# The first modulation's columns in four column groups of the array, as plain 32-bit products

## The chip, the cores and the metric

The kernel runs on one core of a Trainium2 chip. The metric is the device time of one execution in microseconds (us). The core has five engines that run beside each other and meet at semaphores: TensorE (PE in the profile, with PEld for its weight loads), VectorE (DVE), ScalarE (ACT), GpSimd (POOL) and SyncE (SP), which here issues most DMAs.

## The reference, cut to what matters

One layer of a hybrid attention and retention network over 1024 latent and 256 context tokens of width 1024. It begins with a modulation: a vector for each of the two kinds of token goes through SiLU and a 1024 x 6144 matrix, and its first two sixths shift and scale the normalised tokens, from which everything else is computed.

```python
c_silu = jax.nn.silu(c)[:, None, :]
cctx_silu = jax.nn.silu(c_ctx)[None, :]
sh1, sc1, g1, sh2, sc2, g2 = jnp.split(c_silu @ w_ada[l] + b_ada[l], 6, axis=-1)
csh1, csc1, ... = jnp.split(cctx_silu @ w_ada[l] + b_ada[l], 6, axis=-1)
hx = _modulate(_rmsnorm(x, norm1_g[l]), sh1, sc1)      # h * (1 + scale) + shift
hc = _modulate(_rmsnorm(ctx, norm1_g[l]), csh1, csc1)
(xq, xk, xv, ...) = jnp.split(hx @ w_in[l], IN_OFFSETS, axis=-1)
```

All data are 32-bit floats.

## The kernel before

Large products are made from two parts: a number is split into a high part in the format `float32r`, and the low rest, and three such products are summed (`mm3`, `chain`). A product of plain `float32` operands needs no split; the kernel uses it for small things.

The stage that matters is the start, up to about 80 us of the span. Its instructions stand in an order written out by hand (`tc.manual_schedule`), one call after the other, and each engine takes its own instructions in that order. There:

- `load_x`, `square_x`, `rstd_x`, `scale_x` bring a block of 128 tokens (ten of them) and normalise it: DMA by SP, squares on ACT, the root on POOL, the scaling on DVE. `transp` turns its 128 x 128 blocks on PE into PSUM tiles `tp`, `c0` and `c1`; `evac_t` copies some of them out.
- The two conditioning vectors stand as columns, `ccol`: 128 partitions x 8 blocks x 2 vectors. `silu_cc` puts them through SiLU on ACT.
- The modulation's columns (shift and scale) come in four groups `g`, each for two of the eight 128-wide blocks of the width. A group's weights come in four loads `load_ag(g, q)` of 512 KB. The 1024 columns of such a load hold two blocks `k` of the summed dimension, 512 result columns for each.
- `ag_mm(g, q)` multiplies: the vectors are the stationary operand, the weights stream. For groups 0 and 1 (`g < NEX`) these are plain products of two columns by 512, for groups 2 and 3 the weights are split by `ag_hi` (ACT) and `ag_lo` (DVE) into tiles `agh` and `agl`, the vectors by `split_cc` into four columns `ccr`, and two `float32r` products are made for each block.
- `ag_ev` copies the sums from PSUM (`arow`), `ag_tr` turns them into columns (a transpose for groups 0 and 1; for 2 and 3 a product with `sel`, which adds the high and low rows), and `ag_fin` adds the bias and multiplies by the gain, on DVE, into `acol`.
- With a block's shift and scale, `mod_h` (ACT), `mod_v` and `mod_l` (DVE) make the modulated block's high and low parts, and `first_mm(half, kb)` multiplies them on PE by the first weights, whose parts `split_hi` and `split_lo` make.

The last two steps need every earlier one: `first_mm(0, 0)` waits for group 0 of the modulation and for the split weights, and after it PE goes through the sixteen `first_mm` in order, with transposes, `ag_mm` and `ag_tr` between them. SP's DMAs go through eight semaphores in turn, so a load is issued when the one eight places ahead has landed, and the tile that it fills is free.

Of the kernel before, what the change touches and what calls it, by code (L numbers as in the profile page):

```python
# [8 lines left out]
F32 = mybir.dt.float32  # L9
F32R = mybir.dt.float32r  # L10
AF = mybir.ActivationFunctionType
ALU = mybir.AluOpType
# [4 lines left out]
P = 128  # L17
D = 1024
KB = D // P
# [21 lines left out]
def tile_hybrid_layer(ctx, tc: tile.TileContext, io, dbg=None):  # L41
    nc = tc.nc
    vec, act, pool, pe, sync = nc.vector, nc.scalar, nc.gpsimd, nc.tensor, nc.sync

    def sb(name, side, bufs=1):
        return tc.alloc_tile_pool(name=name, bufs=bufs, side=side, reuse_waits="tile")
# [31 lines left out]
    ident = cpool.tile([P, P], F32, name="ident")  # L78
# [72 lines left out]
    s0 = sb("start", "right")  # L151
# [12 lines left out]
    def square_x(tb):  # L164
        act.activation(s_tile("v", 1), xs[tb], AF.Square, accum_out=ssq[:, tb : tb + 1])
# [6 lines left out]
    def scale_x(tb):  # L172
        vec.tensor_scalar(xs[tb], xs[tb], rstd[:, tb : tb + 1], None, ALU.mult)
# [13 lines left out]
    def p_tile(tag):  # L187
        return p0.tile([P, 512], F32, tag=tag, bufs=2 if tag == "tp" else 3, name=tag)
# [14 lines left out]
    copy = {"act": act.copy, "vec": vec.tensor_copy}  # L203
    moved = set()

    def evac_t(grid, half, kb, eng):
        moved.add((grid, half, kb))
        x = xT[grid, kb, half]
        copy[eng](x, tps[grid, half, kb][:, : x.shape[-1]])
# [8 lines left out]
    def mod_h(grid, half, kb):  # L218
        h = hxp(0, kb, half * 512, 512) if grid else hcp(0, kb, 0, C)
        a, sh = (cx if grid else ca)[kb]  # L220
        act.activation(h, turned(grid, half, kb), AF.Identity, bias=sh, scale=a)

    def mod_v(grid, half, kb, v=None):
        modv[grid, half, kb] = s_tile("vh", 3, 512) if v is None else v
        vec.tensor_scalar(modv[grid, half, kb], turned(grid, half, kb), *(cx if grid else ca)[kb], ALU.mult, ALU.add)

    def mod_l(grid, half, kb):
        lo = low(grid, half, kb, F32R)
        h = hxp(0, kb, half * 512, 512) if grid else hcp(0, kb, 0, C)
        vec.tensor_tensor(lo, modv[grid, half, kb], h.bitcast(F32), ALU.subtract)  # L230
        (hx if grid else hc)[1][kb, half] = lo

    ccol = s0.tile([P, KB, 2], F32, name="ccol")
    cs2 = csp.tile([P, D], F32, name="cs")

    def load_cc():
        sync.dma_start(ccol, io["ccol"])

    def silu_cc():
        act.activation(ccol, ccol, AF.Silu)

    def load_bc():
        sync.dma_start(cs2, io["cvec"][0:1].to_broadcast([P, D]))
# [1 line left out]
    def silu_bc():  # L247
        act.activation(cs2, cs2, AF.Silu)

    ag, agh, agl, arow, arow_s, acolT = {}, {}, {}, {}, {}, {}
    ccr = s0.tile([P, KB, 4], F32R, name="ccr")
    sel = s0.tile([4, 2], F32, name="sel")
    NEX = 2

    def load_ag(g, q):
        ag[g, q] = s_tile("x", 14)
        sync.dma_start(ag[g, q], io["w_ada1g"][g, q])

    def ag_hi(g, q):
        agh[g, q] = s0.tile([P, D], F32R, tag="ahl", bufs=6, name="agh")
        act.copy(agh[g, q], ag[g, q])

    def ag_lo(g, q):
        agl[g, q] = s0.tile([P, D], F32R, tag="ahl", bufs=6, name="agl")
        vec.tensor_tensor(agl[g, q], ag[g, q], agh[g, q].bitcast(F32), ALU.subtract)

    def split_cc():
        act.copy(ccr[:, :, 0:2], ccol)  # L270
        vec.tensor_tensor(ccr[:, :, 2:4], ccol, ccr[:, :, 0:2].bitcast(F32), ALU.subtract)
        vec.tensor_tensor(sel, ident[:4, 0:2], ident[:4, 2:4], ALU.add)

    def ag_mm(g, q):
        if q == 0:
            arow[g] = p_tile("tp")
        for e in range(2):
            k, es = 2 * q + e, slice(e * 512, e * 512 + 512)
            if g < NEX:
                pe.matmul(arow[g][:2], ccol[:, k], ag[g, q][:, es], start=k == 0, stop=k == KB - 1)  # L280
            else:
                pe.matmul(arow[g][:4], ccr[:, k], agh[g, q][:, es], start=k == 0, stop=False)
                pe.matmul(arow[g][:4], ccr[:, k], agl[g, q][:, es], start=False, stop=k == KB - 1)

    def ag_ev(g, eng):
        n = 2 if g < NEX else 4
        arow_s[g] = s0.tile([4, 512], F32, tag="arow", bufs=1, name="arow")[:n]
        copy[eng](arow_s[g], arow[g][:n])

    def ag_tr(g):  # L290
        acolT[g] = p_tile("tp")
        for n in range(4):
            o, a = acolT[g][:, 2 * n : 2 * n + 2], arow_s[g][:, n * P : n * P + P]
            if g < NEX:
                pe.transpose(o, a, ident[:2, :2])
            else:
                pe.matmul(o, a, sel, start=True, stop=True)

    def ag_fin(g):
        kbs = slice(2 * g, 2 * g + 2)  # L300
        t = acol[:, :, kbs].rearrange("p s k i -> p i k s")
        bb = cst["b"][:, 0:16].rearrange("p (i k) -> p i k", i=2)
        vec.tensor_tensor(t, acolT[g][:, 0:8].rearrange("p (i k s) -> p i k s", i=2, k=2), bb[:, :, kbs].unsqueeze(3).to_broadcast([P, 2, 2, 2]), ALU.add)
# [20 lines left out]
    def split_lo(half, t):  # L324
        vec.tensor_tensor(first[t][half][:, 1], fraw[half, t], first[t][half][:, 0].bitcast(F32), ALU.subtract)
# [296 lines left out]
    def next_load(i):  # L622
        nraw[i] = rawload(io["w_qkv"][1, 0, i])
# [26 lines left out]
    with tc.manual_schedule():  # L650
        load_ag(0, 0)
        load_cc()
        load_x(0)
        load_x(1)
        silu_cc()
        split_cc()
# [177 lines left out]
        ag_hi(2, 2)  # L834
        ag_lo(2, 2)
        load_ag(3, 2)
        load_ag(3, 3)
        load_bc()
        load_ex()
        next_load(0)  # L840
        ag_hi(2, 3)
        ag_lo(2, 3)
        ag_mm(2, 0)
        ag_mm(2, 1)
        first_mm(1, 2)
# [3 lines left out]
        transp(7, (5,), ("tp",))  # L849
        ag_mm(2, 2)  # L850
        ag_mm(2, 3)
        ag_hi(3, 0)
        ag_lo(3, 0)
        silu_bc()
        evac_t(True, 1, 5, "act")
        ag_hi(3, 1)
        split_lo(1, 1)
        scale_x(9)
        scale_x(8)
        ag_lo(3, 1)  # L860
        ag_ev(2, "act")
        split_hi(1, 0)
        split_lo(1, 0)
        ag_hi(3, 2)
        first_mm(1, 3)
        ag_tr(2)
        ag_fin(2)
        ag_mm(3, 0)
        ag_mm(3, 1)
# [3 lines left out]
        mod_h(True, 1, 4)  # L873
        mod_v(True, 1, 4)
        mod_l(True, 1, 4)
        ag_lo(3, 2)
        ag_hi(3, 3)
        ag_lo(3, 3)
        first_mm(0, 4)
        transp(8, (2,), ("tp",))  # L880
        transp(9, (2,), ("tp",))
# [615 lines left out]
    for db in range(KB):  # L1497
# [4 lines left out]
        for half in range(2):  # L1502
# [21 lines left out]
    arow = ap_.tile([32, P], F32, name="arow")  # L1524
# [100 lines left out]
    for kb in range(KB):  # L1625
        t = wop.tile([P, 2, 512], F32R, tag="wo", bufs=KB, name="wo")
# [11 lines left out]
    for kb in (6, 7, 0, 1, 2, 3, 4, 5):  # L1638
        t = (wop if kb >= 6 else op).tile([P, 2, 512], F32R, tag="wx", bufs=2, name="wx") if kb >= 4 else None
# [475 lines left out]
```

## Time and profile before

| | us |
|---|---|
| median of three runs | 1742.88 |
| lowest and highest | 1742.45, 1744.89 |
| the profiled execution | 1742.64 |
| its span, first to last instruction | 1740.9 |
| PE, DVE, ACT, POOL busy in the span | 1721.2, 1225.3, 846.9, 537.9 |

The span leaves out 1.74 us of the execution's own time. PE is called busy in 99% of the span, but its matmuls are pipelined and the ends of them are modelled: a row of 0.39 us may be followed by the next after 0.23. How long a stream of matmuls takes is therefore read from the starts of its rows, and not from the durations. A plain 32-bit matmul of the program appears as two rows, each with a weight load of its own. In a row of the timeline the first number is the start from the span's begin, the second the duration (of a merged group, from its first start to its last end), and the bracket holds the idle time of the engine before it and what ended it.

### The profile page before, as it was taken

How to read it: one execution, taken by the hardware profiler on the slowest of the kernel's cores; microseconds unless marked ns; L12 is line 12 of the kernel's file. 1: busy time of each engine (PE TensorE's matmuls, PEld its weight loads, DVE VectorE, ACT ScalarE, POOL GpSimd, SP SyncE). 2: the span in 40 equal slices, each digit the busy share in tenths (PEclk: the TensorE clock that was granted, in tenths of full speed). 3: DMA queues.
4: the chain of work that ended last, by engine and by line, in shares of the span. 5: the costliest groups of instructions: out<-in, count | busy, mean ns of one | idle time of the engine just before them, and what ended most of it. 6: DMA issues, size and time to landing. Idle time of an engine off the chain costs nothing.

```text
span 1740.9 us, 25068 instructions
## 1 busy us (share of the span) xinstructions
PE 1721.2 (99%) x8405; PEld 1426.1 (82%) x8405; DVE 1225.3 (70%) x2460; ACT 846.9 (49%) x1803; POOL 537.9 (31%) x703
## 2 busy tenths in 40 slices
PE   8999999999999999999999999999999999999998
PEld 4788888888888887888888888888888888888886
DVE  4877887765776666765555557876888898856756
ACT  5756666563443434443444323544444444545444
POOL 1100001002343344512222211012566666421444
PEclk9999999999999999999999999999999999999999
DMA  8254445542231223578876566768666676898744
GB/s 341 84 162 146 125 144 173 157 125 49 79 89 51 80 43 94 167 260 276 267 226 233 196 196 193 256 215 224 176 197 169 187 209 167 254 318 289 242 152 178
DMA packets 141361, 313.02 MB, mean 180 GB/s; under 512 B 19024, under 2 KB 31472, under 8 KB 135024
## 3 DMA queue, kind: packets, MB, share of 16 engines
q1 hardware_dynamic: 116896, 230.40, 38.4%
q0 software_dynamic: 12032, 70.27, 18.0%
q10 hardware_dynamic: 12304, 10.75, 1.8%
q8 instruction: 66, 1.08, 0.2%
q14 instruction: 63, 0.52, 0.1%
HBM read 250.78 MB, written 121.91 MB: 214 GB/s over the span
## 4 chain that ended last, share of the span: by engine, by line
PE 81%; DMA 5%; issue 5%; DVE 4%; POOL 3%; ACT 2%; SPq 0%; POOLq 0%; ACTq 0%; DVEq 0%
PE u L1377 29%; PE mm L126 4%; PE mm L124 4%; PE mm L125 4%; PE mm L115 3%; PE mm L113 3%; PE mm L114 3%; PE y L1377 2%; PE R L514 2%; PE om L125 2%; PE om L124 2%; PE om L126 2%; PE pr L114 2%; PE pr L113 2%; PE pr L115 2%
## 5 line engine op out<-in xcount | busy, mean ns | idle before, releaser
L1377 PE MATMUL u<-T,wc 128*128 128x512 f32 x960 | 225.0, 390 | 0.3 <-ACT pu L1411 0.2
L1377 PEld LDWEIGHTS u<-T,wc 128*128 128x128 f32 x960 | 179.5, 188 | 39.7 <-ACT pu L1411 2.5
L1377 PE MATMUL y<-wc,ahl 128*128 128x512 f32 x924 | 210.1, 389 | 0.4 <-DVE wc L90 0.4
L1377 PEld LDWEIGHTS y<-wc,ahl 128*128 128x128 f32 x924 | 173.3, 188 | 36.8 <-DVE wc L90 0.8
L90 DVE TENSOR_TENSOR wc<-ur,wc 128x512 fp32r<-128x512 f32 x161 | 118.2, 737 | 62.9 <-ACT wc L89 61.0
L89 ACT CAST wc<-ur 128x512 fp32r<-128x512 f32 x161 | 99.7, 621 | 119.2 <-PE u L1377 69.3
L114 PE MATMUL mm<-low,wc 128*128 128x512 f32 (+1 forms) x312 | 119.1, 382 | 0.0
L1377 PE MATMUL u<-h2a,wc 128*128 128x512 f32 x480 | 112.4, 389 | 0.0
L113 PE MATMUL mm<-hx,wc 128*128 128x512 f32 x264 | 107.3, 406 | 0.2 <-ACT wc L627 0.2
L115 PE MATMUL mm<-hx,wc 128*128 128x512 f32 x264 | 105.7, 401 | 0.0
L1377 PEld LDWEIGHTS u<-h2a,wc 128*128 128x128 f32 x480 | 90.0, 188 | 19.2 <-DVE pu L1420 0.4
L1377 PE MATMUL u<-hxT,wc 128*128 128x512 f32 x384 | 89.6, 389 | 0.0
L585 POOL COPY pad<-pu 128x1 f32<-128x1 f32 x54 | 35.8, 662 | 166.6 <-DVE pu L1414 123.1
L585 POOL COPY pad<-st 128x1 f32<-128x1 f32 x32 | 5.9, 185 | 258.5 <-DVE st L488 258.5
L1377 PEld LDWEIGHTS u<-hxT,wc 128*128 128x128 f32 x384 | 72.1, 188 | 14.9
L89 ACT CAST wc<-raw 128x512 fp32r<-128x512 f32 x86 | 53.1, 621 | 40.1 <-PE pr L115 9.7
L90 DVE TENSOR_TENSOR wc<-raw,wc 128x512 fp32r<-128x512 f32 x86 | 60.5, 708 | 12.1 <-ACT wc L89 8.6
L126 PE MATMUL mm<-wc,low 128*128 128x512 f32 (+1 forms) x180 | 68.8, 382 | 0.0
L89 ACT CAST wc<-s 128x512 fp32r<-128x512 f32 x56 | 34.8, 622 | 68.6 <-PE u L1377 66.4
L114 PEld LDWEIGHTS mm<-low,wc 128*128 128x128 f32 x312 | 58.9, 189 | 7.1
L89 ACT CAST wc<-wr 128x512 fp32r<-128x512 f32 x56 | 34.7, 622 | 56.3 <-PE u L1377 47.2
L1377 PE MATMUL u<-hx,wc 128*128 128x512 f32 x192 | 61.9, 390 | 0.0
(412 smaller groups left out, 4752.8 us busy)
## 6 DMA issues: line engine op xcount, KB each, us to landing
d_a<-at SPq DMA_DIRECT2D x77, 256.0 KB, 6.3
ur<-d_a SPq DMA_DIRECT2D x77, 256.0 KB, 5.3
ur<-in_w_up SPq DMA_DIRECT2D x74, 256.0 KB, 5.8
d_w<-in_w_down POOLq DMA_DIRECT2D x66, 256.0 KB, 7.2
aw<-in_w_ada SPq DMA_DIRECT2D x32, 512.0 KB, 3.9
d_a<-d_a POOLq DMA_DIRECT2D x44, 256.0 KB, 7.3
ur<-d_w SPq DMA_DIRECT2D x44, 256.0 KB, 3.8
d_s<-in_w_up POOLq DMA_DIRECT2D x36, 256.0 KB, 6.0
```

Of the source, the lines that this page charges most:

```text
L89: act.copy(hi, src)
L90: (lo_eng or vec).tensor_tensor(lo, src, hi.bitcast(F32), ALU.subtract)
L113: pe.matmul(out, wh, xh, start=k == 0, stop=False)
L114: pe.matmul(out, wh, xl, start=False, stop=False)
L115: pe.matmul(out, wl, xh, start=False, stop=k == n - 1)
L124: pe.matmul(out, ah, bh, start=first, stop=False)
L125: pe.matmul(out, ah, bl, start=False, stop=False)
L126: pe.matmul(out, al, bh, start=False, stop=last)
L514: pe.matmul(R[:, h], self.pair.V[:, g, h].rearrange("p a b -> p (a b)"), self.PT[h][:, c].rearrange("p a b -> p (a b)"), start=c == 0, sto ...
L585: late(pool.tensor_copy(tick, src))
L1377: pe.matmul(out, a, b, start=first and n == 0, stop=last and n == 2, skip_group_check=True)
```

## The change

All four groups are now made by plain 32-bit products. The stationary operand is padded from two columns to 32 with zeros (`ccol`, cleared once by DVE; the vectors land in `ccin`, and SiLU writes them into its first two columns). The 1024 columns of a load are multiplied as four pieces of 256, and each piece goes to a column group of its own: 32 columns of the array, and the 32 partitions of the PSUM tile that belong to them. The sums then stand in 128 partitions x 256 instead of 2 or 4 x 512; `sel` has a one where a row belongs to a vector and half, and two products with it turn and add them in one step. The splits `ag_hi`, `ag_lo` and `split_cc` are gone from the order; every other call stays where it was.

```diff
-    ccol = s0.tile([P, KB, 2], F32, name="ccol")
+    ccin = s0.tile([P, KB, 2], F32, name="ccin")
+    ccol = s0.tile([P, KB, 32], F32, name="ccol")
+    vec.memset(ccol, 0.0)
...
-        act.activation(ccol, ccol, AF.Silu)
+        act.activation(ccol[:, :, 0:2], ccin, AF.Silu)
...
-    def ag_hi(g, q):
-        agh[g, q] = s0.tile([P, D], F32R, tag="ahl", bufs=6, name="agh")
-        act.copy(agh[g, q], ag[g, q])
-
-    def ag_lo(g, q):
-        agl[g, q] = s0.tile([P, D], F32R, tag="ahl", bufs=6, name="agl")
-        vec.tensor_tensor(agl[g, q], ag[g, q], agh[g, q].bitcast(F32), ALU.subtract)
...
+    def make_sel():
+        a, b = (ident[:, c : c + 64].rearrange("p (i c) -> p i c", i=2)[:, :, 0:2] for c in (0, 64))
+        vec.tensor_tensor(sel.rearrange("p (i s) -> p i s", i=2), a, b, ALU.add)
...
-        for e in range(2):
-            k, es = 2 * q + e, slice(e * 512, e * 512 + 512)
-            if g < NEX:
-                pe.matmul(arow[g][:2], ccol[:, k], ag[g, q][:, es], start=k == 0, stop=k == KB - 1)
-            else:
-                pe.matmul(arow[g][:4], ccr[:, k], agh[g, q][:, es], start=k == 0, stop=False)
-                pe.matmul(arow[g][:4], ccr[:, k], agl[g, q][:, es], start=False, stop=k == KB - 1)
+        for n in range(4):
+            k, r = 2 * q + n // 2, slice(32 * n, 32 * n + 32)
+            pe.matmul(arow[g][r, 0:256], ccol[:, k], ag[g, q][:, n * 256 : n * 256 + 256], start=q == 0, stop=q == 3, tile_position=(0, 32 * n))
...
-        copy[eng](arow_s[g], arow[g][:n])
+        arow_s[g] = s0.tile([P, 256], F32, tag="arow", bufs=1, name="arow")
+        copy[eng](arow_s[g], arow[g][:, 0:256])
...
-        for n in range(4):
-            o, a = acolT[g][:, 2 * n : 2 * n + 2], arow_s[g][:, n * P : n * P + P]
-            if g < NEX:
-                pe.transpose(o, a, ident[:2, :2])
-            else:
-                pe.matmul(o, a, sel, start=True, stop=True)
+        for k in range(2):
+            pe.matmul(acolT[g][:, 4 * k : 4 * k + 4], arow_s[g][:, k * P : k * P + P], sel, start=True, stop=True)
...
         mod_l(True, 1, 2)
-        ag_hi(2, 0)
         mod_v(True, 1, 3)
         mod_h(True, 1, 3)
-        ag_lo(2, 0)
-        ag_hi(2, 1)
         mod_l(True, 1, 3)
-        ag_lo(2, 1)
         first_mm(1, 1)
```

On PE, the place between the second and the third `first_mm` of the second half, where `ag_mm(2, 0)` and `ag_mm(2, 1)` stand. Before (`agh` and `agl` are the weights' parts, `c_...` the sums of `first_mm`; the last number is partitions x columns):

```order
L126 MATMUL c_481<-hx_130,wc 128x8x8x8
L282 MATMUL tp<-agh,ccr 4x512
L283 MATMUL tp<-agl,ccr 4x512
L282 MATMUL tp<-agh,ccr 4x512
L283 MATMUL tp<-agl,ccr 4x512
L282 MATMUL tp<-agh,ccr 4x512
L283 MATMUL tp<-agl,ccr 4x512
L282 MATMUL tp<-agh,ccr 4x512
L283 MATMUL tp<-agl,ccr 4x512
L124 MATMUL c_479<-hx_134,wc 128x8x8x8
```

The same place on PE after the change (`x` is the tile into which the weights landed):

```order
L126 MATMUL c_492<-hx_130,wc 128x8x8x8
L270 MATMUL tp<-x,ccol 32x256 x8
L124 MATMUL c_490<-hx_134,wc 128x8x8x8
L125 MATMUL c_490<-low,wc 128x8x8x8
L126 MATMUL c_490<-hx_134,wc 128x8x8x8
```

Eight single matmuls of 512 columns have become eight double ones of 256 columns, at four positions of the array in turn, and they read the loaded tile itself. On DVE a little before and behind that place, first before the change:

```order
L230 TENSOR_TENSOR low<-vh,hx_134 128x512
L225 TENSOR_SCALAR vh<-low,acol 128x512
L267 TENSOR_TENSOR agl<-x,agh 128x1024
L230 TENSOR_TENSOR low<-vh,hx_138 128x512
L267 TENSOR_TENSOR agl<-x,agh 128x1024 x4
L325 TENSOR_TENSOR wc<-raw,wc 128x512
L173 TENSOR_SCALAR x<-x,rstd 128x1024 x2
```

And after it, on DVE (`low` are blocks' low parts, `wc` the first weights' parts):

```order
L230 TENSOR_TENSOR low<-vh,hx_134 128x512
L225 TENSOR_SCALAR vh<-low,acol 128x512
L230 TENSOR_TENSOR low<-vh,hx_138 128x512
L307 TENSOR_TENSOR wc<-raw,wc 128x512
L173 TENSOR_SCALAR x<-x,rstd 128x1024 x2
```

The five subtractions of the splits have gone, and nothing else changed its place; three more stand further on, and ACT loses its eight casts in the same way.

More of the change, by code (lines that the diff above doesn't have):

```diff
@@ L231, in mod_l @@
         (hx if grid else hc)[1][kb, half] = lo
-    ccol = s0.tile([P, KB, 2], F32, name="ccol")
+    ccin = s0.tile([P, KB, 2], F32, name="ccin")
+    ccol = s0.tile([P, KB, 32], F32, name="ccol")
+    vec.memset(ccol, 0.0)
     cs2 = csp.tile([P, D], F32, name="cs")
     def load_cc():
-        sync.dma_start(ccol, io["ccol"])
+        sync.dma_start(ccin, io["ccol"])
     def silu_cc():
-        act.activation(ccol, ccol, AF.Silu)
+        act.activation(ccol[:, :, 0:2], ccin, AF.Silu)
     def load_bc():
@@ L248, in silu_bc @@
         act.activation(cs2, cs2, AF.Silu)
[L252 to L255, printed above, removed]
+    ag, arow, arow_s, acolT = {}, {}, {}, {}
+    sel = s0.tile([P, 4], F32, name="sel")
     def load_ag(g, q):
@@ L259, in load_ag @@
         sync.dma_start(ag[g, q], io["w_ada1g"][g, q])
-    def ag_hi(g, q):
-        agh[g, q] = s0.tile([P, D], F32R, tag="ahl", bufs=6, name="agh")
-        act.copy(agh[g, q], ag[g, q])
-    def ag_lo(g, q):
-        agl[g, q] = s0.tile([P, D], F32R, tag="ahl", bufs=6, name="agl")
[L267 to L272, printed above, removed]
+    def make_sel():
+        a, b = (ident[:, c : c + 64].rearrange("p (i c) -> p i c", i=2)[:, :, 0:2] for c in (0, 64))
+        vec.tensor_tensor(sel.rearrange("p (i s) -> p i s", i=2), a, b, ALU.add)
     def ag_mm(g, q):
@@ L276, in ag_mm @@
             arow[g] = p_tile("tp")
-        for e in range(2):
-            k, es = 2 * q + e, slice(e * 512, e * 512 + 512)
-            if g < NEX:
-                pe.matmul(arow[g][:2], ccol[:, k], ag[g, q][:, es], start=k == 0, stop=k == KB - 1)
-            else:
-                pe.matmul(arow[g][:4], ccr[:, k], agh[g, q][:, es], start=k == 0, stop=False)
-                pe.matmul(arow[g][:4], ccr[:, k], agl[g, q][:, es], start=False, stop=k == KB - 1)
+        for n in range(4):
+            k, r = 2 * q + n // 2, slice(32 * n, 32 * n + 32)
+            pe.matmul(arow[g][r, 0:256], ccol[:, k], ag[g, q][:, n * 256 : n * 256 + 256], start=q == 0, stop=q == 3, tile_position=(0, 32 * n))
     def ag_ev(g, eng):
-        n = 2 if g < NEX else 4
-        arow_s[g] = s0.tile([4, 512], F32, tag="arow", bufs=1, name="arow")[:n]
-        copy[eng](arow_s[g], arow[g][:n])
+        arow_s[g] = s0.tile([P, 256], F32, tag="arow", bufs=1, name="arow")
+        copy[eng](arow_s[g], arow[g][:, 0:256])
     def ag_tr(g):
         acolT[g] = p_tile("tp")
-        for n in range(4):
-            o, a = acolT[g][:, 2 * n : 2 * n + 2], arow_s[g][:, n * P : n * P + P]
-            if g < NEX:
-                pe.transpose(o, a, ident[:2, :2])
-            else:
-                pe.matmul(o, a, sel, start=True, stop=True)
+        for k in range(2):
+            pe.matmul(acolT[g][:, 4 * k : 4 * k + 4], arow_s[g][:, k * P : k * P + P], sel, start=True, stop=True)
     def ag_fin(g):
@@ L302, in ag_fin @@
         bb = cst["b"][:, 0:16].rearrange("p (i k) -> p i k", i=2)
-        vec.tensor_tensor(t, acolT[g][:, 0:8].rearrange("p (i k s) -> p i k s", i=2, k=2), bb[:, :, kbs].unsqueeze(3).to_broadcast([P, 2, 2, 2]), ALU.add)
+        vec.tensor_tensor(t, acolT[g][:, 0:8].rearrange("p (k i s) -> p i k s", i=2, k=2), bb[:, :, kbs].unsqueeze(3).to_broadcast([P, 2, 2, 2]), ALU.add)
         vec.tensor_tensor(t[:, 1], t[:, 1], cst["g"][:, 0, kbs].unsqueeze(2).to_broadcast([P, 2, 2]), ALU.mult)
@@ L655, in tile_hybrid_layer @@
         silu_cc()
-        split_cc()
+        make_sel()
         square_x(0)
@@ L840, in tile_hybrid_layer @@
         next_load(0)
-        ag_hi(2, 3)
-        ag_lo(2, 3)
         ag_mm(2, 0)
@@ L851, in tile_hybrid_layer @@
         ag_mm(2, 3)
-        ag_hi(3, 0)
-        ag_lo(3, 0)
         silu_bc()
         evac_t(True, 1, 5, "act")
-        ag_hi(3, 1)
         split_lo(1, 1)
@@ L859, in tile_hybrid_layer @@
         scale_x(8)
-        ag_lo(3, 1)
         ag_ev(2, "act")
@@ L863, in tile_hybrid_layer @@
         split_lo(1, 0)
-        ag_hi(3, 2)
         first_mm(1, 3)
@@ L875, in tile_hybrid_layer @@
         mod_l(True, 1, 4)
-        ag_lo(3, 2)
-        ag_hi(3, 3)
-        ag_lo(3, 3)
         first_mm(0, 4)
```

2 lines of the change are left out of this document (removed).

## Prediction

> **What bounds the kernel now.** I read the page first, then the engines' busy time by stage, then the rows of PE, DVE and SP in the start, and last the chain of waits. The page:
>
> ```profile
> PE 81%; DMA 5%; issue 5%; DVE 4%; POOL 3%; ACT 2%; SPq 0%; POOLq 0%; ACTq 0%; DVEq 0%
> ```
>
> PE carries the chain that ends last. The change touches only the start, so the stages there decide (us, then busy time by engine with its instructions, PE's granted clock, DMA share, GB/s):
>
> ```profile
> 13.40:29.10 15.70, 15.69 (x61) 5.58 (x60) 7.84 (x13) 9.48 (x17) 1.71 (x4) 1.00 0.94 365
> 29.10:46.10 17.00, 16.62 (x88) 13.27 (x88) 12.96 (x21) 12.92 (x22) 3.16 (x5) 1.00 0.94 357
> 46.10:67.40 21.30, 21.07 (x102) 13.62 (x100) 18.32 (x32) 14.62 (x20) 2.73 (x3) 1.00 0.12 38
> ```
>
> PE is the fullest engine in all three; up to 46 us the DMAs are nearly as full, behind it DVE is. After 67.4 us everything hangs on group 3's columns, so a microsecond won or lost before them should reach the end.
>
> PE's rows of the first two groups show what a plain product costs:
>
> ```profile
> 4.49 3.57 PE L280 MATMUL tp<-x,ccol 128*2 128x512 f32 x4 [4.49 <-ACT ccol L242]
> 9.92 3.57 PE L280 MATMUL tp<-x,ccol 128*2 128x512 f32 x4 [1.86 <-DMA x<-in_w_ada1g]
> ...
> 14.27 1.88 PE L280 MATMUL tp<-x,ccol 128*2 128x512 f32 x4
> 16.08 0.33 PE L201 MATMUL c<-ident,x 128*128 128x128 f32 x1
> ...
> 17.43 1.88 PE L280 MATMUL tp<-x,ccol 128*2 128x512 f32 x4
> 19.24 1.09 PE L201 MATMUL c<-ident,x 128*128 128x128 f32 x8
> ...
> 20.37 0.41 PE L295 MATMUL tp<-ident,arow 2*128 2x2 f32 x4
> 20.71 0.33 PE L201 MATMUL c<-ident,x 128*128 128x128 f32 x1
> 21.04 3.59 PE L280 MATMUL tp<-x,ccol 128*2 128x512 f32 x8
> 24.57 0.44 PE L201 MATMUL c<-ident,x 128*128 128x128 f32 x2
> ...
> 27.33 1.88 PE L280 MATMUL tp<-x,ccol 128*2 128x512 f32 x4
> 29.14 0.50 PE L124 MATMUL c<-hx,wc 128*128 128x512 f32 x1
> 29.48 0.39 PE L125 MATMUL c<-low,wc 128*128 128x512 f32 x1
> 29.70 0.40 PE L126 MATMUL c<-hx,wc 128*128 128x512 f32 x1
> ```
>
> Four passes hold PE 1.81 us (14.27 to 16.08), eight 3.53 (21.04 to 24.57): 0.43 a pass, and 0.09 for the step to the next kind. Behind a plain product the first split one takes 0.34 to the next row where the second takes 0.22, so the step back costs 0.12 more. A plain product of 512 columns is two passes, 0.86 us. The first two loads' passes take twice that, before PE has been busy for long.
>
> **The change, part by part.** *Split products become plain ones in groups 2 and 3.* PE's rows there, and the turns (L297):
>
> ```profile
> 46.09 0.40 PE L282 MATMUL tp<-agh,ccr 128*4 128x512 f32 x1
> ...
> 47.64 0.40 PE L283 MATMUL tp<-agl,ccr 128*4 128x512 f32 x1 [0.23 <-DVE agl L267]
> ...
> 48.34 0.39 PE L124 MATMUL c<-hx,wc 128*128 128x512 f32 x1
> ...
> 50.75 0.47 PE L282 MATMUL tp<-agh,ccr 128*4 128x512 f32 x1
> ...
> 52.68 0.39 PE L124 MATMUL c<-hx,wc 128*128 128x512 f32 x1
> ...
> 54.82 1.05 PE L297 MATMUL tp<-sel,arow 4*128 4x2 f32 x8
> 55.80 0.39 PE L282 MATMUL tp<-agh,ccr 128*4 128x512 f32 x1
> ...
> 57.64 0.39 PE L124 MATMUL c<-hx,wc 128*128 128x512 f32 x1
> ...
> 62.44 0.39 PE L282 MATMUL tp<-agh,ccr 128*4 128x512 f32 x1
> ...
> 64.29 0.39 PE L124 MATMUL c<-hx,wc 128*128 128x512 f32 x1
> ...
> 66.42 1.05 PE L297 MATMUL tp<-sel,arow 4*128 4x2 f32 x8
> 67.40 0.66 PE L201 MATMUL tp<-ident,x 128*128 128x128 f32 x4
> ```
>
> Each visit of PE makes two loads' products: 2.25, 1.93, 1.84 and 1.85 us, 7.87 in all. After the change a visit is eight plain products of 256 columns, sixteen passes of 0.43 / 2 = 0.215 us. One after the other they take 3.44. Were all four column groups to run at once, a load's four products would take the time of one, 0.43, and a visit 0.86. No row of before has two column groups, so these are the ends. I take a value between, for this reason: the two passes of one product add into the same place and follow each other, and if PE begins its passes in the order of the program, the first pass of the next group can begin only with the second pass of this one. Then one pass in two is covered, n products take n + 1 passes, and a visit takes 9 x 0.215 = 1.94.
>
> The Trainium skill says on this (TensorE: Matmul & The Clock Gate, Part 3) that matmuls at different column positions run beside each other, three of them measured at 2.38 times the speed, and that all start and end in program order; whether plain 32-bit passes do so, no row here shows.
>
> Four visits: 4 x 1.94 = 7.74. Stepping in and out of the plain kind, free for split products, costs 0.09 in, 0.09 out and 0.12 on the next row: 0.30 for three visits and, behind `ag_tr`, 0.21 for the third: 1.11. So +0.98 against 7.87, the vanished wait of 0.23 for `agl` included. The turns shrink from four products to two: 54.82 to 55.80 and 66.42 to 67.40 are 0.98 each, halved, -0.98 together. Groups 2 and 3 come to about **0.0**, with -0.5 to +0.6 for the entries.
>
> *The splits go.*
>
> ```profile
> L267 DVE TENSOR_TENSOR agl<-x,agh 128x1024 fp32r<-128x1024 f32 x8 | 9.4, 1217 | 0.6 <-ACT agh L263 0.6
> ...
> L263 ACT CAST agh<-x 128x1024 fp32r<-128x1024 f32 x8 | 8.2, 1049 | 0.3 <-PE tp L282 0.2
> ```
>
> That frees 9.4 us of DVE and 8.2 of ACT, but PE waited for it 0.23 us only, already counted. What the splits read is late next: the loads, issued long before. I give this nothing more.
>
> *Groups 0 and 1 in column groups.* A load's product goes from eight half passes to five: 0.64 us less at full speed, 1.3 at the slow one. Between 9.92 and `ag_fin(0)` lie one slow and two fast ones, 2.6 us. But others bound this:
>
> ```profile
> 16.05 0.75 DVE L173 TENSOR_SCALAR x<-x,rstd 128x1024 f32<-128x1024 f32 x1 [1.97 <-POOL rstd L170]
> ...
> 20.81 0.17 DVE L303 TENSOR_TENSOR acol<-tp,bcol 128x8 f32<-128x8 f32 x1 [4.01 <-PE tp L295]
> ...
> 22.09 0.81 DVE L225 TENSOR_SCALAR vh<-c,acol 128x512 f32<-128x512 f32 x1 [0.91 <-ACT hx L221]
> ...
> 27.43 0.69 DVE L209 COPY low<-tp 128x512 f32<-128x512 f32 x1 [0.49 <-PE tp L201]
> 28.04 0.68 DVE L325 TENSOR_TENSOR wc<-raw,wc 128x512 fp32r<-128x512 f32 x1
> ```
>
> The fourth block is scaled at 16.80, and its nine transposes and the turn follow, 1.57 us from 19.24 to 20.81, plus 0.15 for the costlier turn (0.49 instead of 0.34, 20.37 to 20.71): not before 18.5, so at most 2.3. I take 1.8, for a clock that quickens later. From `ag_fin(0)` on ACT and then DVE (22.09) work without a break up to the split's end at 28.72, but for the 0.49 in which DVE waits for transposes; those stand behind a product and come earlier. So `first_mm(0, 0)` may begin at 28.72 - 0.49 - 1.8 = 26.4 instead of 29.14: -2.7. PE is ready by then, since four products of group 1 give back 2.6 too. Taken off: 0.15 for group 1's turn and 0.2 for the context blocks, whose loads are issued behind DVE's splits. **-2.3**, with 0.9 and 3.3 as bounds.
>
> The clearing of `ccol` and the making of `sel` lie in DVE's idle time before 9 us, and the evictions behind transposes or a `first_mm`; without that cover they would cost some tenths.
>
> **Sum:** -2.3 + 0.0 on the profiled execution's 1742.64 (0.24 below the median of the runs, which I leave): **1740.3 us**, -0.13%. About 0.2%, 3.5 us, is what a measurement of this kernel tells from no change.
>
> **The rivals.**
>
> *No overlap (slower).* If the column groups' passes run one after the other, groups 2 and 3 cost 4 x 3.44 + 1.11 - 7.87 - 0.98 = +6.0, and the first two gain nothing and pay 0.15 for the turn: 1748.8. For it: successive passes in the trace never come closer than 0.43 us; against it, all of them use one position. It turns the sign once a visit takes about 2.5 us, since 4 x 0.57 over the 1.94 eat the 2.3.
>
> *No overlap, and a stop at every change of position.* At 0.09 to 0.29 for each of 64 products, +6 to +19 more: 1754 and over. Nothing in the rows speaks for it but those steps.
>
> *All four at once (faster).* Group 2's and 3's visits shrink to 0.86 us, 3.44 + 1.11 - 7.87 - 0.98 = -4.3, of which about 1 is lost at 57.64, where `first_mm(0, 4)` would wait for DVE's low part; the start gains 2.5: 1736.8. The Trainium skill (TensorEngine Tiling (Array Packing), Theoretical Speedup) gives up to four times for at most 32 columns. Against it stands the order of the two passes.
>
> *Weight loads show.* A load of a new position may not begin until the second pass has:
>
> ```profile
> L280 PEld LDWEIGHTS tp<-x,ccol 128*2 128x2 f32 x32 | 2.3, 89 | 16.7 <-issue 8.2 <-ACT ccol L242 4.5 <-DMA x<-in_w_ada1g 3.6
> ...
> L297 PEld LDWEIGHTS tp<-sel,arow 4*128 4x128 f32 x16 | 1.9, 186 | 0.7 <-issue 0.7
> ```
>
> Loads of 2 and of 128 columns take 89 and 186 ns; with 110 for 32, a visit is 7 x 0.325 + 0.43 = 2.7, groups 2 and 3 +3.1, the start -1.9: 1743.8.
>
> *The clock stays slow.* The passes at 9.92 take twice those at 14.27. Fewer passes may leave PE slow for longer. The third load has landed by
>
> ```profile
> 12.50 0.33 SPq L94 DMA_DIRECT2D raw<-in_w_qkv  x1
> ```
>
> the issue that waits for it. PE's work from 14.27 to 29.14 is 14.9 us, less 6 x 0.64 it is 11.0: begun at 12.5 and at twice the time throughout, it ends at 34.5, 5.4 late; if PE quickens half way, at 29.0. I take +2.5: 1745.1. The Trainium skill (TensorE: Matmul & The Clock Gate, Part 1) has PE at half rate until some 3.4 us of sustained work; the trace agrees in kind, with 3.57 us rows before the quick ones.
>
> **How the numbers follow.** Forecast 0.38, no overlap 0.24, with stops 0.08, all at once 0.14, weight loads 0.11, clock 0.05. The forecast's own range is 1738.8 to 1742.0. The range 1736.5 to 1749.5 takes in all but the stops and the tails of the two outer cases. Faster by over 0.2% are all at once and a quarter of the forecast, 0.23; slower the two without overlap and the dear ends of the next two, 0.35; within 0.2% the rest, 0.42.
>
> **What would show it.** Right: the start of the first `L270` row at group 2 to the next `L124` row is near 2.2 us with the steps, `first_mm(0, 0)` begins near 26.5, and `ag_tr(3)` ends some 2.3 us before 67.40. Visits near 3.7 mean no overlap, near 1.1 all four at once; starts of passes 0.1 us late behind weight loads, or passes of 0.43 us past 15 us, mean the last two. The reading as a whole is wrong if `ag_tr(3)` moved and the end does not.

## The result and the profile after

The changed kernel takes 1737.64 us, median of seven runs (1735.53 to 1739.17); the kernel before took 1742.88 beside it, also a median of seven (1740.48 to 1747.88). The ratio is 0.9965, 95% interval 0.9952 to 0.9978: about 6 us faster (the two medians lie 5.2 apart). The range held that. The likeliest case (1740.3) did not come about; what came about is the rival in which all four column groups work at once (1736.8).

The profiled execution took 1738.69 us, its span is 1736.9. The chain that ended last, from the page of the kernel after, is still PE's:

```profile
PE 80%; issue 5%; DMA 5%; DVE 5%; POOL 3%; ACT 2%; SPq 0%; POOLq 0%; ACTq 0%; DVEq 0%
```

The three stretches of the start again, kernel after (same columns as before):

```profile
13.40:29.10 15.70, 12.07 (x99) 7.61 (x92) 9.65 (x19) 9.86 (x18) 1.88 (x5) 1.00 1.02 397
29.10:46.10 17.00, 16.77 (x101) 12.44 (x103) 12.74 (x25) 11.92 (x21) 2.70 (x4) 1.00 0.93 361
46.10:67.40 21.30, 20.77 (x136) 15.57 (x132) 13.51 (x29) 11.68 (x19) 0.26 (x1) 1.00 0.04 13
```

In the first stretch PE was busy all the time before; now it has gaps of 3.6 us in all, while the DMAs are busy throughout. What the gaps wait for stands in PE's rows of the kernel after, up to the first products with split weights:

```profile
5.89 1.08 PE L270 MATMUL tp<-x,ccol 128*32 128x256 f32 x8 [5.89 <-ACT ccol L244]
10.24 1.08 PE L270 MATMUL tp<-x,ccol 128*32 128x256 f32 x8 [3.27 <-DMA x<-in_w_ada1g]
...
12.85 1.08 PE L270 MATMUL tp<-x,ccol 128*32 128x256 f32 x8 [0.26 <-DMA x<-in_w_ada1g]
...
15.51 0.64 PE L270 MATMUL tp<-x,ccol 128*32 128x256 f32 x8
17.17 1.09 PE L201 MATMUL c<-ident,x 128*128 128x128 f32 x8 [1.02 <-DVE x L173]
...
18.21 0.51 PE L279 MATMUL tp<-sel,arow 128*128 128x4 f32 x4
...
22.69 0.64 PE L270 MATMUL tp<-x,ccol 128*32 128x256 f32 x8 [0.27 <-DMA x<-in_w_ada1g]
23.26 0.50 PE L124 MATMUL c<-hx,wc 128*128 128x512 f32 x1
...
26.14 0.50 PE L126 MATMUL c<-hx,wc 128*128 128x512 f32 x1 [1.46 <-DVE wc L307]
```

A load's product took 1.81 us to the next row before, at full speed; with its eight passes of 256 columns it takes 0.57 now (22.69 to 23.26). PE then waits for loads, for the scaling of the fourth block, for a copy by ACT (0.63 ahead of 21.05), and for the last split of the first weights. The four visits for groups 2 and 3 and the two turns (L279), kernel after:

```profile
42.23 1.07 PE L270 MATMUL tp<-x,ccol 128*32 128x256 f32 x16
43.23 0.50 PE L124 MATMUL c<-hx,wc 128*128 128x512 f32 x1
...
45.96 1.07 PE L270 MATMUL tp<-x,ccol 128*32 128x256 f32 x16
46.96 0.50 PE L124 MATMUL c<-hx,wc 128*128 128x512 f32 x1
...
49.15 0.50 PE L279 MATMUL tp<-sel,arow 128*128 128x4 f32 x4
49.58 1.07 PE L270 MATMUL tp<-x,ccol 128*32 128x256 f32 x16
50.96 0.50 PE L124 MATMUL c<-hx,wc 128*128 128x512 f32 x1 [0.31 <-ACT hx L221]
...
56.23 1.07 PE L270 MATMUL tp<-x,ccol 128*32 128x256 f32 x16
57.23 0.50 PE L124 MATMUL c<-hx,wc 128*128 128x512 f32 x1
...
59.41 0.50 PE L279 MATMUL tp<-sel,arow 128*128 128x4 f32 x4
59.77 0.63 PE L201 MATMUL tp<-ident,x 128*128 128x128 f32 x4
```

Visits take 1.00, 1.00, 1.38 and 1.00 us. The first starts 3.86 us earlier than before (42.23 against 46.09), and the row behind group 3's turn 7.63 earlier (59.77 against 67.40). So the start gave 3.86 and the stage of groups 2 and 3 gave 3.77: visits 4.38 instead of 7.87 (-3.49), turns 0.43 and 0.36 instead of 0.98 each (-1.17), and 0.89 paid outside the visits, for stepping in and out and for waits.

Of those 7.63 us 4.0 are left at the end of this profiled span (1736.9 against 1740.9). How much of that loss is real is taken up with the last experiment but one.

### The profile page after: what moved, and what is told of

It reads as the page before. It is cut to its first block, busy times and chain, and to the rows that moved or that the text cites. A ratio compares the mean times of both kernels' runs of the same rounds, so it can differ in the third digit from the quotient of the medians.

```text
span 1736.9 us, 25158 instructions
## 1 busy us (share of the span) xinstructions
PE 1708.0 (98%) x8461; PEld 1423.4 (82%) x8461; DVE 1219.5 (70%) x2452; ACT 839.2 (48%) x1794; POOL 540.1 (31%) x703
## 3 DMA queue, kind: packets, MB, share of 16 engines
q8 instruction: 66, 1.08, 0.2%
## 4 chain that ended last, share of the span: by engine, by line
PE 80%; issue 5%; DMA 5%; DVE 5%; POOL 3%; ACT 2%; SPq 0%; POOLq 0%; ACTq 0%; DVEq 0%
PE u L1343 29%; PE mm L126 4%; PE mm L124 4%; PE mm L125 4%; PE mm L115 3%; PE mm L114 3%; PE mm L113 3%; PE y L1343 2%; PE R L496 2%; PE ptp L478 2%; PE pr L114 2%; PE pr L113 2%; PE pr L115 2%; PE om L125 1%; PE om L124 1%
## 5 line engine op out<-in xcount | busy, mean ns | idle before, releaser
L90 DVE TENSOR_TENSOR ahl<-ur,ahl 128x512 fp32r<-128x512 f32 x66 | 52.4, 802 | 11.4 <-ACT ahl L89 11.2
```

The source lines that it names most:

```text
L90: (lo_eng or vec).tensor_tensor(lo, src, hi.bitcast(F32), ALU.subtract)
```

## The experiments

One table for all; "turn done" is the start of the row behind group 3's turn in the profiled run, "rest" what follows it to the end of the span. The ratios are to the kernel before on the same chip.

| kernel | turn done, us | span | rest | ratio (95%) |
|---|---|---|---|---|
| before | 67.40 | 1740.9 | 1673.5 | |
| after | 59.77 | 1736.9 | 1677.1 | 0.9965 (0.9952-0.9978) |
| late_only | 61.94 | 1735.9 | 1674.0 | 0.9970 (0.9958-0.9982) |
| early_only | 63.36 | 1737.8 | 1674.4 | 0.9980 (0.9972-0.9989) |
| one_position | 70.81 | 1746.4 | 1675.6 | 1.0034 (1.0020-1.0047) |
| position_pairs | 59.07 | 1735.4 | 1676.3 | 0.9965 (0.9952-0.9978) |
| late_table | 65.72 | 1740.0 | 1674.3 | 0.9988 (0.9979-0.9997) |
| early_table | 59.59 | 1736.4 | 1676.8 | 0.9956 (0.9942-0.9969) |
| reordered | 59.93 | 1736.3 | 1676.4 | 0.9958 (0.9945-0.9970) |
| after_again | 59.82 | 1736.0 | 1676.2 | 0.9954 (0.9941-0.9966) |
| before_again | 67.10 | 1742.4 | 1675.3 | 0.9995 (0.9984-1.0007) |
| position_quads | 65.14 | 1740.8 | 1675.7 | 0.9998 (0.9986-1.0010) |

**late_only: column groups for groups 2 and 3 alone.** From the kernel after, groups 0 and 1 go back to two columns by 512:

```diff
     def ag_mm(g, q):
+        if g < 2:
+            for e in range(2):
+                k, es = 2 * q + e, slice(e * 512, e * 512 + 512)
+                pe.matmul(arow[g][:2], ccol[:, k, 0:2], ag[g, q][:, es], start=k == 0, stop=k == KB - 1)
+            return
...
```

> Groups 0 and 1 as before, groups 2 and 3 in four column groups without splits. Theory A (passes of the four column groups run at once, a visit takes 1.0 us): the four visits fall from 7.87 to about 4.0 us, the two turns from 0.98 to 0.4 each, about 0.5 is lost where the third visit waits for the modulated block, so the first transpose after the last turn starts near 62.8 instead of 67.40, and the time falls by 3 to 4.6 us. Theory B (the forecast's: one pass in two is covered): visits of 2.2 us, that transpose within 0.6 us of 67.4, time as before.

PE's rows of late_only, the second product of group 0, the first visit and the end:

```profile
10.14 1.88 PE L271 MATMUL tp<-x,ccol 128*2 128x512 f32 x4 [0.79 <-DMA x<-in_w_ada1g]
...
27.62 0.50 PE L124 MATMUL c<-hx,wc 128*128 128x512 f32 x1
...
44.35 1.07 PE L275 MATMUL tp<-x,ccol 128*32 128x256 f32 x16
45.35 0.50 PE L124 MATMUL c<-hx,wc 128*128 128x512 f32 x1
...
61.94 0.63 PE L201 MATMUL tp<-ident,x 128*128 128x128 f32 x4
```

The visits are as short as in the kernel after. But `first_mm(0, 0)` too starts 1.52 us earlier than before (27.62 against 29.14), though its products are those of before: the second product, 3.57 us long before, takes 1.88. Of the 5.46 us at the turn, 3.94 are then the column groups' in groups 2 and 3. late_table, below, looks for the 1.5.

**early_only: column groups for groups 0 and 1 alone.** From the kernel before; groups 2 and 3 keep their splits:

```diff
     def ag_mm(g, q):
+        if g < NEX:
+            for n in range(4):
+                k, r = 2 * q + n // 2, slice(32 * n, 32 * n + 32)
+                pe.matmul(arow[g][r, 0:256], cpad[:, k], ag[g, q][:, n * 256 : n * 256 + 256], start=q == 0, stop=q == 3, tile_position=(0, 32 * n))
+            return
...
```

> Groups 0 and 1 in column groups, groups 2 and 3 split as before. Theory A: the product of groups 2 begins near 42.5 instead of 46.09 as in the changed kernel, the last turn ends about 3.5 us before 67.40, and the time falls by 2.5 to 3.5 us. Theory B: 2.3 us. Were the start bounded by the loads alone, under 1 us.

The turn is done 4.04 us earlier than before. 3.94 and 4.04 add up to 7.98, the kernel after has 7.63: the two halves of the change stand beside each other and nearly add.

**one_position: no splits and no column groups.** From the kernel after, all four groups are plain products of two columns by 512, at one position:

```diff
-        for n in range(4):
-            k, r = 2 * q + n // 2, slice(32 * n, 32 * n + 32)
-            pe.matmul(arow[g][r, 0:256], ccol[:, k], ..., start=q == 0, stop=q == 3, tile_position=(0, 32 * n))
+        for e in range(2):
+            k, es = 2 * q + e, slice(e * 512, e * 512 + 512)
+            pe.matmul(arow[g][:2], ccol[:, k, 0:2], ag[g, q][:, es], start=k == 0, stop=k == KB - 1)
...
```

> All four groups by plain products of two columns by 512 at one position, no splits and no column groups. Theory A (the gain is the overlap of the column groups): visits of 3.5 us, the start as before, the last turn ends 5 to 6.5 us after 67.40, time near 1748.6. Rival (the gain is what the splits free on ScalarE and VectorE): the last turn not later than 67.40 and time at or under 1742.9.

A visit of one_position in PE's rows:

```profile
43.96 3.59 PE L270 MATMUL tp<-x,ccol 128*2 128x512 f32 x8
47.49 0.50 PE L124 MATMUL c<-hx,wc 128*128 128x512 f32 x1
```

It lasts 3.53 us where the kernel after takes 1.00, with as many columns streamed, and the kernel is slower than before, with the same splits gone. So the gain is not the freed DVE and ACT; it is the work at four positions at once. The turn is 3.41 us later than before, less than the 5 to 6.5 expected, for the start is quicker here too: the second product takes 2.02 us where it had 3.57 (late_table, below).

**position_pairs: how PE gets at the other positions.** From the kernel after: in groups 2 and 3 the products of one position stand behind each other, for both loads of a visit, so that three passes of the same position follow each first one:

```diff
+        if g > 1:
+            if q % 2:
+                for n in range(4):
+                    r = slice(32 * n, 32 * n + 32)
+                    for u in (q - 1, q):
+                        pe.matmul(arow[g][r, 0:256], ccol[:, 2 * u + n // 2], ag[g, u][:, n * 256 : n * 256 + 256], ..., tile_position=(0, 32 * n))
+            return
```

> The changed kernel, but in groups 2 and 3 the products of a visit's two loads at one position follow each other directly (0 0 1 1 2 2 3 3 instead of 0 1 2 3 0 1 2 3). If each position works off its own passes and PE looks ahead over the waiting ones (theory A1): visits stay at 1.0 us and the time is that of the changed kernel. If passes begin in program order and only neighbours at different positions run together (theory A2): 13 of 16 passes follow each other, visits of 2.8 to 2.9 us, the last turn ends about 7.4 us later than in the changed kernel's profile (59.77), and the time is 5 to 7 us over the changed kernel's.

The first visit of position_pairs:

```profile
41.45 1.09 PE L273 MATMUL tp<-x,ccol 128*32 128x256 f32 x16
42.48 0.50 PE L124 MATMUL c<-hx,wc 128*128 128x512 f32 x1
```

It takes 1.03. The starts of the sixteen single passes in the two traces, in us, a column for each position:

```
after            42.229 42.235 42.242 42.249     position_pairs   41.455 41.468 41.482 41.495
                 42.469 42.475 42.482 42.489                      41.695 41.708 41.722 41.735
                 42.684 42.691 42.698 42.704                      41.911 41.924 41.937 41.951
                 42.900 42.907 42.914 42.920                      42.127 42.140 42.153 42.167
```

The rows don't name a pass's position; the columns are read from the order and the spacing. Two passes of the program before each change of position give steps of 6 to 7 ns between first passes, four give 13 to 14. In position_pairs the program reads down the columns. So read, the fifth pass of the program starts 13 ns behind the first, and 0.23 us ahead of the second. A pass that waits for its own position does not hold up those behind it.

**position_quads: how far that reaches.** All four loads of group 2 (and of group 3) in one visit, position by position: seven passes of the same position follow each first one. The diff is that of position_pairs with `if q == 3` and `for u in range(4)`.

> The changed kernel, but in groups 2 and 3 all four loads' products stand in one visit, ordered by position: eight passes of one position, then eight of the next. If PE looks over all waiting passes: 32 passes in four at a time, a visit of 1.8 to 1.9 us. If it looks ahead over fewer than 24 waiting passes, positions start later, up to 8 + 3 x 7 = 29 passes in a row: 2.5 to 6.3 us.

The visit and the turn behind it, in PE's rows of position_quads:

```profile
44.25 4.59 PE L273 MATMUL tp<-x,ccol 128*32 128x256 f32 x32
48.77 0.50 PE L124 MATMUL c<-hx,wc 128*128 128x512 f32 x1
...
50.97 0.50 PE L286 MATMUL tp<-sel,arow 128*128 128x4 f32 x4
52.78 0.50 PE L124 MATMUL c<-hx,wc 128*128 128x512 f32 x1 [1.31 <-ACT hx L221]
```

4.52 us for 32 passes: one after the other they would take 6.9, four at once 1.7. The starts of the passes (while two positions work, each one's starts follow each other after 0.215 us and lie 0.03 from the other's, which tells them apart):

```
position 1   44.249 44.490 44.706 44.922 45.137 45.353 45.569 45.785
position 2   45.143 45.383 45.599 ...
position 3   46.037 46.277 ...
position 4   46.930 47.170 ...                          last 48.465
```

Each position begins 6 ns after the fifth pass of the one before, when three of that one's passes are left. That fits one pass at work and three waiting for each position: 3 x 0.893 until the fourth begins, and 8 x 0.215 for its passes, 4.40, and 0.12 to the next row. It is the forecast's idea of a blocked order after all, but four passes deep and not one; the kernel after, with two passes before the position changes, never meets it.

**late_table: the 1.5 us of late_only.** The kernel before, with only this:

```diff
+    ccin = s0.tile([P, KB, 2], F32, name="ccin")
     ccol = s0.tile([P, KB, 2], F32, name="ccol")
+    vec.memset(ccol, 0.0)
...
-        act.activation(ccol, ccol, AF.Silu)
+        act.activation(ccol, ccin, AF.Silu)
```

> The kernel before, with one thing of the change alone: the conditioning vectors land in a tile of their own, and the tile that SiLU writes is cleared first by VectorE, so that ScalarE's load of its function table waits for the vectors too. Theory C (the later first product lets PE's clock quicken before the second): the first product starts at 5.8 instead of 4.49, the second runs in 1.88 instead of 3.57 us, the last turn ends 1.5 to 1.9 us before 67.40, and the time falls by 1 to 2 us. Rival (the 1.5 to 1.9 us that two kernels with unchanged early products had won at 20 us come from their missing split of the vectors, or from chance): the second product takes 3.57 us, no lead, time as before.

ACT's first rows, kernel after (late_table has the same two within 0.02 us of these):

```profile
4.33 1.28 ACT L244 ACT_TABLE_LOAD   x1 [4.33 <-DMA ccin<-in_ccol]
5.62 0.22 ACT L244 ACTIVATE ccol<-ccin 128x16 f32<-128x16 f32 x1
```

In the trace before, the load of the table lay at 0.74, ahead of the wait for the vectors. In late_table the load of the table waits for the vectors, and SiLU ends 1.4 us later. That the second producer (the clearing on DVE) does it, and not the separate tile, is argued: the two came together in every run. PE's rows of late_table show where the time is won:

```profile
5.88 3.57 PE L282 MATMUL tp<-x,ccol 128*2 128x512 f32 x4 [5.88 <-ACT ccol L244]
10.08 2.16 PE L282 MATMUL tp<-x,ccol 128*2 128x512 f32 x4 [0.62 <-DMA x<-in_w_ada1g]
```

PE stood still for 0.62 us ahead of the second product, where before it had been 1.86, and that product takes 2.16 us instead of 3.57 (1.88 in late_only, after 0.79). The turn is done 1.68 us earlier, and the ratio's interval lies just below one. That is a side effect of the change that the prediction overlooked. But the shorter pause is not shown to be its cause: in before_again, the unchanged kernel's second trace, PE stood still for 2.09 us and was quick all the same, and lost it again. Its second product, and two stretches from 11 us on, with PE's granted clock as the third number from the end:

```profile
10.16 2.31 PE L280 MATMUL tp<-x,ccol 128*2 128x512 f32 x4 [2.09 <-DMA x<-in_w_ada1g]
```

```profile
11.00:12.00 1.00, 1.00 (x3) 0.09 (x1) 0.75 (x1) 0.51 (x1) 0.12 (x1) 0.74 1.06 415
12.00:13.00 1.00, 1.00 (x4) 0.60 (x4) 0.09 (x1) 0.64 (x2) 0.19 (x2) 0.50 1.04 418
```

The speed of the passes goes with the trace's records of the granted clock. In before_again they say full from 8.07 us, half from 11.48 to 14.89, then full again. In the other eleven traces PE's passes take about twice the time up to the first record, which says full, and run at full speed behind it. It begins at 13.79 us in before; at 9.36, 10.03 and 10.68 in late_only, one_position and late_table; at 13.83 in the kernel after, and at 14.74 to 15.97 in the six others with column groups in groups 0 and 1, after_again among them. Ahead of the first record there is none, and a view prints 1.00 there: that is no sign of full speed.

So the 1.5 us come from an earlier full speed. Three of three kernels with plain products of two columns that begin at 5.8 to 5.9 us had it by 10.7. But the kernel before, which begins them at 4.5, had it at 13.79 in one trace and for a time at 8.07 in the other: what sets the moment stays open.

**early_table: the same in the kernel after.** A SiLU of one column ahead draws the table in early:

```diff
+        act.activation(s0.tile([P, 1], F32, name="warm"), mhalf[:, 0:1], AF.Silu)
         act.activation(ccol[:, :, 0:2], ccin, AF.Silu)
```

> The changed kernel with a SiLU of one column ahead, which draws the table load to the begin. Theory: the first products start near 4.5 instead of 5.89, but the second ones wait for their load as before (10.2), so group 0 is ready no earlier, the last turn ends within 0.4 us of the changed kernel's 59.77, and the time is that of the changed kernel. Rival (the late table load costs the changed kernel its 1.3 us): the last turn ends near 58.4, time 1 us less.

The first product starts at 4.64 instead of 5.89, the second at 10.07 for its load; the turn is done at 59.59 against 59.77, the ratio is that of after_again (0.9956 and 0.9954). In the kernel after, where PE waits for loads and DVE in the start, the late table costs and wins nothing that shows.

**reordered: the wait of 1.46 us ahead of the sixth row of `first_mm(0, 0)`.** On DVE the last split of the first weights moves ahead of `mod_v` and `mod_l` of the second block and of an eviction, and `ag_ev(1)` and `scale_x(4)` move with it:

```diff
         split_lo(0, 0)
+        split_lo(0, 1)
         mod_h(True, 0, 1)
...
         evac_t(True, 0, 6, "vec")
-        split_lo(0, 1)
         first_mm(0, 0)
```

> The changed kernel with VectorE's order changed in four places: the last split of the first weights and the eviction of group 1 ahead of the second modulated block, the scaling of block 4 ahead of the block's values for the third. Theory (VectorE bounds the first product of the hidden state now, 1.46 us of waiting): that wait goes, the transposes of blocks 4 and 5 begin 0.5 to 1.5 us earlier than the changed kernel's 29.88, the last turn ends 0.5 to 1.2 us earlier, and the time falls by as much. Rival (the squares on ScalarE are late next): the transposes begin at 29.5 or later and the time is the changed kernel's.

The wait is gone and others came, reordered's PE rows:

```profile
29.00 0.33 PE L201 MATMUL c<-ident,x 128*128 128x128 f32 x1 [0.37 <-DVE x L173]
...
31.00 0.55 PE L201 MATMUL c<-ident,x 128*128 128x128 f32 x3 [1.01 <-DVE vh L225]
31.30 0.47 PE L124 MATMUL c<-hx,wc 128*128 128x512 f32 x1
```

The transposes start at 29.00 against 29.88 in the kernel after, but the last three wait for `mod_v` on DVE, and the `first_mm` behind them starts at 31.30 against 30.95. The next bound took over at once; the turn is done at 59.93 against 59.77.

**after_again and before_again: what is lost behind the start.** Both kernels unchanged, traced once more.

> The changed kernel itself, on the same chip as the other three. Theory D (what is lost behind 1100 us of the lead at the end of the start is landing times that differ from run to run): the lead over the profile of before at 1099 us is 6 to 8 us again, and what is left at the end differs from the first profile's 3.9 us. Theory E (an earlier start always gives it back there): 3.9 us are left again. The time over that of before: a ratio between 0.995 and 0.998.

> The kernel before once more, for its trace. Theory D (the stages behind 1000 us differ from run to run, and the first profile of before was a quick one there): from the last turn's end to the end of the span this profile takes longer than the first one's 1673.5 us (1740.9 less 67.40), by 1 us or more. Theory E (an earlier start gives lead back there): 1673.5 within 0.5 us.

The same code before takes 1673.5 and 1675.3 us behind the turn: 1.8 us apart. So the comparison with the first trace of before overstates the loss; against before_again the two traces of the kernel after keep 5.5 and 6.4 us at the end of the span. A part looks real: the five kernels that are done with the turn before 60 us have rests of 1676.2 to 1677.1, the other seven of 1673.5 to 1675.7. But these are single traces, and the run times don't bear it out: by their ratios early_table, reordered and after_again gain 7.7, 7.3 and 8.0 us, give or take 2.4, and their leads at the turn over the first trace of before are 7.8, 7.5 and 7.6.

One wait that could lose time is that of the first product with `kH`, in the kernel after:

```profile
92.30 0.35 PE L457 MATMUL sl<-kH,qS 128*128 128x256 f32 x1 [1.14 <-DMA kH<-kH]
```

It is 0.26 and 0.22 in the two traces of before, and 1.14, 0.78, 0.63, 0.31 and 0.22 in after, early_table, reordered, position_pairs and after_again. The kernel after has the longest and the shortest of these, and position_pairs, which comes earliest, waits only 0.31: the wait differs from trace to trace, and an early start is not shown to lengthen it. Most of what differs comes later: the last 4000 matmul rows of PE and what follows them, from about 1050 us on, take 688.0 and 690.0 us in the traces of before, 690.4 to 691.0 in the five, and 688.8 to 690.4 in the remaining five. How much of the lead the change loses behind the start, if any, stays open.

No version beat the kernel after: position_pairs, early_table and reordered have its ratio within their intervals.

## Why the prediction was right in its range and wrong in its likeliest case

That the time lies in the range is owed to its width: it reached down to this rival, at 1736.5, while the forecast's own range, 1738.8 to 1742.0, missed.

**The step that failed** is "if PE begins its passes in the order of the program, the first pass of the next group can begin only with the second pass of this one". PE does not: the first passes of four positions start 7 ns apart, the second passes 0.24 later. A visit took 1.00 us, not 1.94; one_position and position_pairs show that the positions do it and that their order in the program does not matter at this depth. The rival with that mechanism held 0.14; it was set low for a rule on the order of passes that no row showed.

**Groups 2 and 3**: forecast 0.0, the rival -4.3 with 1 us of it lost, measured -3.77. The loss sits where it was put, at `first_mm(0, 4)` (50.96 now): 0.31 for ACT's part at its first row, and 0.2 more for DVE's low part, half of the 1 us named. The steps in and out were counted at 1.11. Of that, 0.36 (0.09 at the end of each visit) lies inside what is called a visit here; 0.75 stands against the 0.89 outside. The visits took 4.38 where the rival's 3.44 and these 0.36 make 3.80; most of the rest is the third visit, with its wait. The turns were halved in the sum, -0.98; measured -1.17.

**The start**: -2.3 with -3.3 as its far end, measured -3.86, outside the bounds. The chain was right: group 0's columns came 2.06 us earlier (18.75 against 20.81; forecast 1.8) and the first weights' last split ended at 26.09 against 28.72, -2.63 against -2.3. The mis-sized step is "`first_mm(0, 0)` may begin at 28.72 - 0.49 - 1.8": only its sixth row needs that split. Five rows went ahead from 23.26, while before all nine stood behind PE's own products. That sixth row in the kernel before:

```profile
30.40 0.39 PE L126 MATMUL c<-hx,wc 128*128 128x512 f32 x1
```

Counted there the lead is 30.40 - 26.14 = 4.26, and 0.4 of it went to waits ahead of 42 us. These are DVE's rows of the kernel after on which the start hung, the columns of group 0 first:

```profile
18.75 0.17 DVE L285 TENSOR_TENSOR acol<-tp,bcol 128x8 f32<-128x8 f32 x1 [1.64 <-PE tp L279]
...
25.41 0.68 DVE L307 TENSOR_TENSOR wc<-raw,wc 128x512 fp32r<-128x512 f32 x1
```

**No overlap** did not come. one_position, which has none, is 0.34% slower, near the 0.35% of that rival's 1748.8. Its visits take 3.53 us with a step in them, where 3.44 without one was assumed. At the turn it is only 3.4 us later, thanks to its quicker start; the other 2.1 us of its span come behind the turn, where the rival put none, so the near price is in part luck.

**Weight loads** stayed hidden. All loads of a 32-column operand in the kernel after (count, then shortest, middle and longest in ns):

```profile
L270 PEld LDWEIGHTS tp<-x,ccol x128: 106/110/154, 5.9 to 56.7; 128*32 128x32 f32 x128
```

The 110 ns were right; the loads of four positions start 7 ns apart like the passes.

**The clock**: in this trace PE came to full speed at 13.83 us, as before at 13.79. The third load's product at 12.85 takes 1.08 where those from 15.51 on take 0.64, because it now comes ahead of that moment. In the other six traces with column groups in groups 0 and 1 full speed came at 14.74 to 15.97, later than in the first trace of before, as that rival had it. It cost nothing that shows, since the rows behind wait for loads and for DVE: position_pairs, the last to reach full speed, is the first done with the turn. The +2.5 us of that rival needed PE to be the bound, and with four positions at once it no longer was.

**The splits** were given nothing more than 0.23 us, which one_position bears out: without splits and without column groups the kernel is slower.

## What to carry to other kernels

A product with few stationary columns is worth spreading over the array's column groups: here four positions took 1.00 us for what one position does in 3.53, in 32-bit products too, and PE found the overlap by itself with two and with four passes of a position in a row; with eight it found a part of it only. When one engine's work in a hand-written order shrinks, ask which single row behind it needs the next engine, not when the whole step may begin. A wait can move onto an instruction ahead of the one that needs it, as the load of ACT's table shows. A granted clock of 1.00 ahead of a trace's first clock record says nothing; the spacing of PE's rows does.

## What the runs showed of the hardware

- Passes of different column positions start 6 to 14 ns apart and overtake waiting ones of another position, up to three of them; each position does its own, one every 0.215 us (256 columns). The Trainium skill (TensorE: Matmul & The Clock Gate, Part 3) has all matmuls start in program order; for plain 32-bit products the traces of the kernel after, position_pairs and position_quads differ, and they decide. Four positions gave 3.53 / 1.00 = 3.5 times the speed with the steps in it; up to four is what the Trainium skill (TensorEngine Tiling (Array Packing), Theoretical Speedup) states.
- The same first products of one kernel run at two speeds in two traces: a pass of 512 columns follows the last after 0.85 us or after 0.43. The change comes where a clock record begins: in before at 13.79, behind the second product; in before_again at 8.07, ahead of it, with half the clock again from 11.48 to 14.89, two stretches of 3.41 us. Where the views print 1.00 ahead of the first record, passes take about twice the time.
- A SiLU that reads and writes the tile the vectors land in had its table loaded at 0.74 us, ahead of its wait for them; writing another tile, cleared by DVE, it had the same load wait until 4.33.
